# One-input Newton steps, first weights subtracted on VectorE, and a residual moved behind two projections, in a two-layer decoder trunk

## The chip, the cores and the metric

The kernel runs on one core of a Trainium2 chip. The metric is the device time of one execution in microseconds (us). The engines are TensorE (PE in the profile; its weight loads are PEld), VectorE (DVE), ScalarE (ACT), GpSimd (POOL) and SyncE (SP), which here only issues loads. Each engine works through its own queue in order; semaphores connect the queues.

## The reference

x is 512 tokens by 1024 features, mem is 256 fixed tokens by 1024, everything in float32. After an input norm, two layers follow, each with three sub-layers in the form x <- LayerNorm(alpha * x + f(x)):

```python
def reference(x, mem, ln0_g, ln0_b, ...):
    h = layer_norm(x, ln0_g, ln0_b)
    for l in range(DEPTH):
        mix = hybrid_mixer(h, w_in[l], w_a2[l], b_a[l], conv_w[l], ..., w_mix_out[l])
        h = layer_norm(DEEPNORM_ALPHA * h + mix, ln1_g[l], ln1_b[l])
        xa = memory_cross_attention(h, mem, w_xq[l], w_xkv[l], w_xo[l])
        h = layer_norm(DEEPNORM_ALPHA * h + xa, ln2_g[l], ln2_b[l])
        ff = swiglu(h, w_ffn_in[l], w_ffn_out[l])
        h = layer_norm(DEEPNORM_ALPHA * h + ff, ln3_g[l], ln3_b[l])
    return h

def hybrid_mixer(h, ...):
    c_a, c_g, q, k, v, r, a_low = jnp.split(h @ w_in, cuts, axis=-1)
    u = causal_depthwise_conv(c_a * jax.nn.sigmoid(c_g), conv_w, conv_b)   # 31 taps, 512 channels
    u = jax.nn.silu(layer_norm(u, conv_ln_g, conv_ln_b))
    log_a = jax.nn.log_sigmoid(a_low @ w_a2 + b_a) / GATE_TAU
    o = gla_chunked(q, k, v, log_a)                                        # 4 heads, chunks of 64
    o = rms_norm(o, gla_norm_g) * jax.nn.silu(r)
    return jnp.concatenate([u, o], axis=-1) @ w_out
```

## The kernel before

Every matmul operand is split into a high part, rounded by ScalarE, and a low part, the difference: `split` (lines 100 to 102) is one ScalarE copy and one subtraction on the engine it is given. A product is three matmuls, `mm3` (lines 137 to 139): high by high, high by low, low by high.

Weights come in chunks of 128 x 1024 (512 KB). `wchunk` loads a chunk by SP's queue into one of four `raw` buffers, and splits it into one of four ring buffers (or a resident one). Which engine does the subtraction is a setting, `wlo_engines(...)`: the engines named there take the chunks in turn. It is set to `(POOL, DVE)` for the memory keys `mem_K` of layer 0, to `(POOL)` at the start of each layer's mixer (line 557), to `(POOL, DVE)` after the r projection, and to `(DVE)` for the cross-attention.

Tokens lie in four tiles h[0..3] of 128 x 1024. Large blocks (hT, qk, v, KT, gamma and beta rows `gb`, and so on) come from one pool of 15 equal buffers, `blk`. The instructions are ordered by a planner (the tile framework's scheduler, which plays a model of the engines and takes instructions by the order in which they were written, apart from sections of high or low priority). So the order on a queue can change wherever a change makes something ready earlier or later in that model.

The pieces that the change touches, in the order of the run:

- *Start.* The memory is transposed (mT), `mem_K` makes the keys in four pairs of chunks (w_xk), while the input norm runs at high priority (lines 509 to 528): statistics, `rstd_of`, normalization on ScalarE without gamma and beta, transposes, and per-feature gamma and beta on the transposed side, which gives hT (high and low).
- *The Newton steps.* `rstd_of(v, n, name)` makes 1/sqrt of n columns per token row on VectorE: an integer start (line 147), t = y*v*y (lines 151 to 154), and products of the form (x + c) * z (lines 157, 159, 160). n is 1 for the LayerNorms over tokens, 2 for the convolution's norm, 8 for the RMS norm of the attention.
- *The mixer.* `conv_in(0)` (weights w_c, four chunks: g, then a), `conv_taps(0)` (62 multiply-adds on VectorE at low priority, line 590), `gates()`, `conv_in(1)`, `conv_taps(1)`, the k and q projections (w_qk, four chunks), transposes of kd, the v projection (w_v, four chunks), states S, `gla_pair(0)` with the first half of the r projection (w_r, four chunks), the rest of r, memory values (w_xv, eight chunks), then `conv_norm()` and `gla_pair(1)` at high priority, and the output projection (w_mo), whose results are added to h at line 273.
- *The residual.* The first sub-layer of layer 0 needs the input norm's output with gamma and beta, token-wise. `residual0()` (lines 530 to 534) loads gamma and beta, broadcast to 128 rows, with two loads on SP's queue into one of the 15 buffers, then does four multiplications and four additions of 128 x 1024 on GpSimd. It is called behind the transposes of kd, ahead of the v projection.
- *Between the layers.* The last norm of layer 0 (`layer_norm`, lines 174 to 202, names `y_ln`, `t_ln`, `s_ln`) produces the hT of layer 1, for which `conv_in(0)` of layer 1 waits. That `conv_in` works in two halves of tokens, so its first half needs only the first two token tiles.

Of the kernel before, what the change touches and what calls it, by code (L numbers as in the profile page):

```python
# [17 lines left out]
ALU = mybir.AluOpType  # L18
# [33 lines left out]
def trunk(ctx: ExitStack, tc, a, out):  # L52
    nc = tc.nc
    PE, ACT, DVE, POOL = nc.tensor, nc.scalar, nc.vector, nc.gpsimd
# [18 lines left out]
    def block(shape, dt, name):  # L73
        return blk.tile(shape, dt, tag="b", name=name)
# [25 lines left out]
    def split(hi, lo, src, eng=DVE):  # L100
        ACT.activation(hi, src, AF.Copy)  # L101
        eng.tensor_sub(lo, src, f(hi))  # L102
# [3 lines left out]
    def wlo_engines(*engs):  # L106
        wlo[0], wlo[1] = engs, 0
# [6 lines left out]
    def new_hT(name):  # L114

        return [[block([P, 4, T], F32R, f"hT{j}{i}_{name}") for i in range(2)] for j in range(2)]

    def mov_hT(hT):
        return lambda kt: (hT[0][kt // 4][:, kt % 4, :], hT[1][kt // 4][:, kt % 4, :])
# [21 lines left out]
    def rstd_of(v, n, name):  # L141


        y = small.tile([P, n], F32, tag=f"ny{n}", name=f"y_{name}")
        t = small.tile([P, n], F32, tag=f"nt{n}", name=f"t_{name}")
        s = small.tile([P, n], F32, tag=f"ns{n}", name=f"s_{name}")
        DVE.tensor_scalar(y.bitcast(I32), v.bitcast(I32), -0.5, 1597463007.0 - 2.0 ** 31, ALU.mult, ALU.add)

        def vyy():
            if n > 1:  # L150
                DVE.tensor_mul(t, y, v)
                DVE.tensor_mul(t, t, y)
            else:
                DVE.scalar_tensor_tensor(t, y, v, y, ALU.mult, ALU.mult)

        vyy()
        DVE.scalar_tensor_tensor(y, t, -3.0, y, ALU.add, ALU.mult)
        vyy()
        DVE.scalar_tensor_tensor(s, t, -40.0 / 3.0, t, ALU.add, ALU.mult)
        DVE.scalar_tensor_tensor(y, s, 80.0, y, ALU.add, ALU.mult)  # L160
        return y

    def bcast_row(dst, src_row, n, q):
# [2 lines left out]
    def load_gb(g, b, name, q=nc.sync):  # L166
        gb = block([P, 2, D], F32, f"gb_{name}")
        bcast_row(gb[:, 0, :], g, D, q)
        bcast_row(gb[:, 1, :], b, D, q)
        return gb  # L170
# [4 lines left out]
    def layer_norm(tt, st, gb, name, hT=None, store=None):  # L175
        ht = h[tt]
        mv = small.tile([P, 2], F32, tag="mv", name=f"mv_{name}{tt}")
        DVE.bn_aggr(mv, st)
        v = small.tile([P, 1], F32, tag="v", name=f"v_{name}{tt}")
        DVE.tensor_scalar(v, mv[:, 1:2], EPS, VS, ALU.add, ALU.mult)  # L180
        tail = store is not None and tt == NT - 1
        for i in range(2):
            s = slice(i * 512, (i + 1) * 512)
            DVE.scalar_tensor_tensor(
                ht[:, s], ht[:, s], mv[:, 0:1], gb[:, 0, s], ALU.subtract, ALU.mult)
        y = rstd_of(v, 1, f"{name}{tt}")
        for i in range(2):
            for c0 in range(i * 512, (i + 1) * 512, 256 if tail else 512):
                s = slice(c0, c0 + (256 if tail else 512))
                DVE.scalar_tensor_tensor(ht[:, s], ht[:, s], y, gb[:, 1, s], ALU.mult, ALU.add)  # L190
                if store is not None:
                    (nc.scalar if c0 % 512 else nc.sync).dma_start(store[:, s], ht[:, s])
            if hT is None:
                continue
            pt = bank(f"lt_{name}{tt}_{i}", tag="tr")
            for k in range(4):
                c = (i * 4 + k) * P
                PE.transpose(pt[:, k * P:(k + 1) * P], ht[:, c:c + P], ident)
            pv = pt.rearrange("p (k t) -> p k t", k=4)
            if callable(hT):  # L200
                hT(i, tt, pv)
                continue
            ts_ = slice(tt * P, (tt + 1) * P)
            split(hT[0][i][:, :, ts_], hT[1][i][:, :, ts_], pv)

    def proj_feat(w, mov, specs, name, n=T, halves=False):

        work = []
        for si, (c0, ncol, evac) in enumerate(specs):
            kk = 1024 // ncol  # L210
            wcs = [wchunk(w[ci * kk * P:(ci + 1) * kk * P, c0:c0 + ncol], kk, ncol, f"{name}{si}{ci}")
                   for ci in range(NK // kk)]
            banks = [bank(f"pp_{name}{si}{m}") for m in range(ncol // P)]
            work.append((kk, wcs, banks, evac))
        parts = [(0, n // 2), (n // 2, n)] if halves else [(0, n)]
        for t0, t1 in parts:
            for kk, wcs, banks, evac in work:
                for ci, (wh, wl) in enumerate(wcs):
                    for m, bk in enumerate(banks):
                        ms = slice(m * P, (m + 1) * P)  # L220
                        for k in range(kk):
                            kt = ci * kk + k
                            mh, ml = mov(kt)
                            mm3(bk[:, t0:t1], wh[:, k, ms], wl[:, k, ms], mh[:, t0:t1],
                                ml[:, t0:t1], kt == 0, kt == NK - 1)
                if t1 == n:
                    with tc.high_priority(offset=HP):
                        for m, bk in enumerate(banks):
                            evac(m, bk[:, :n])
# [20 lines left out]
    def run(gen):  # L250
        for _ in gen:
            pass
# [204 lines left out]
    def mem_T(name):  # L457
        mT = [block([P, NK, MEM], F32R, f"mT{j}_{name}") for j in range(2)]
        mraws = block([P, 2, D], F32, f"mem_{name}")
        for mt in range(2):  # L460
            nc.sync.dma_start(mraws[:, mt, :], a["mem"][0, mt * P:(mt + 1) * P, :])
        for mt in range(2):
            mraw = mraws[:, mt, :]
            for i in range(2):
                pt = bank(f"mt{mt}{i}_{name}", tag="tr")
                for k in range(4):
                    PE.transpose(pt[:, k * P:(k + 1) * P], mraw[:, (i * 4 + k) * P:(i * 4 + k + 1) * P], ident)
                ks, ms_ = slice(i * 4, i * 4 + 4), slice(mt * P, (mt + 1) * P)
                split(mT[0][:, ks, ms_], mT[1][:, ks, ms_], pt.rearrange("p (k t) -> p k t", k=4))
        return lambda kt: (mT[0][:, kt, :], mT[1][:, kt, :])  # L470

    def new_K(l):
        return [block([P, NK, MEM], F32R, f"KT{j}_{l}") for j in range(2)]

    def mem_K(l, mT, KT, pr):
        proj_feat(a["w_xkv"][l], mT,
                  [(pr * 256, 256, lambda m, ps: split(KT[0][:, pr * 2 + m, :], KT[1][:, pr * 2 + m, :], ps))],
                  f"xk{pr}_{l}", n=MEM)
# [10 lines left out]
    def load_x(*tts):  # L489
        for tt in tts:  # L490
            nc.sync.dma_start(h[tt], a["x"][0, tt * P:(tt + 1) * P, :])
# [7 lines left out]
    lncol = const.tile([P, 2 * NK], F32, name="lncol")  # L499
    DVE.tensor_copy(lncol, pl[:, :2 * NK])  # L500
    KT = new_K(0)
    mem_K(0, mT, KT, 0)
    load_x(0, 1)
    mem_K(0, mT, KT, 1)
    load_x(2, 3)
    for pr in range(2, 4):
        mem_K(0, mT, KT, pr)
    hT = new_hT("ln0")
# [21 lines left out]
    def residual0():  # L530
        gb = load_gb(a["ln0_g"], a["ln0_b"], "ln0")
        for tt in range(NT):
            POOL.tensor_mul(h[tt], h[tt], gb[:, 0, :])
            POOL.tensor_add(h[tt], h[tt], gb[:, 1, :])
# [4 lines left out]
    for l in range(L):  # L539
# [14 lines left out]
        DVE.tensor_scalar(nba, chan[:, 0:2, CW + 3], -1.0, None, ALU.mult)  # L554
        gnorm = chan[:, 0, CW + 4:CW + 5]
        mov = mov_hT(hT)
        wlo_engines(POOL)


        u = block([P, 4, T], F32, n_("u"))  # L560
# [9 lines left out]
        def conv_in(half):  # L570
            def ev_g(m, ps):
                ACT.activation(u[:, half * 2 + m, :], ps, AF.Sigmoid)

            def ev_a(m, ps):
                DVE.tensor_mul(u[:, half * 2 + m, :], u[:, half * 2 + m, :], ps)

            proj_feat(w_in, mov, [(CD + half * 256, 256, ev_g), (half * 256, 256, ev_a)], n_(f"c{half}"),
                      halves=half == 0 and l > 0)
# [55 lines left out]
            DVE.tensor_copy(dec, qe[:, :, CH - 1::CH])  # L634

        conv_in(0)
        if l > 0:
            mT = mem_T(f"{l}")
            KT = new_K(l)
# [13 lines left out]
        for hp in range(2):  # L653
# [1 line left out]
            for tt in range(NT):  # L655
                PE.transpose(pt[:, tt * P:(tt + 1) * P], kd[:, hp, tt * P:(tt + 1) * P], ident)
            ACT.activation(kdT[:, hp].rearrange("p a b -> p (a b)"), pt, AF.Copy)
        if l == 0:
            residual0()
        v = block([P, NT, 512], F32, n_("v"))  # L660
        run(proj_tok(w_in, mov, 1536, lambda tt, ps: ACT.activation(v[:, tt, :], ps, AF.Copy), n_("v")))

# [3 lines left out]
        for g in range(2):  # L666
# [12 lines left out]
            for cc in range(4):  # L679
                c, pu = g * 4 + cc, pus[cc % 2][:, cc // 2]  # L680
# [116 lines left out]
            mem_K(l, mT, KT, 0)  # L797
        gla_pair(0)
        run(proj_r)
        wlo_engines(POOL, DVE)  # L800
        for pr in range(1, 4) if l > 0 else ():
            mem_K(l, mT, KT, pr)
# [126 lines left out]
```

## Time and profile before

| | before |
|---|---|
| median of 3 runs | 1446.42 us (1444.23 to 1446.85) |
| profiled execution | 1448.14 us, span 1446.4 us |
| TensorE busy | 1405.3 us (97%) |
| VectorE busy | 1015.9 us (70%) |
| ScalarE busy | 608.8 us (42%) |
| GpSimd busy | 218.8 us (15%) |
| granted TensorE clock, mean | 0.992 |

A row of the order of time gives start, duration (both us; for several instructions in a row, from the first's start to the last's end), engine, line, operation, output<-inputs, shapes and count, and in brackets the idle time before it with what ended it. A row of waits gives who waited for what: total us, times, longest. A row of a stretch gives the busy time of PE, PEld, DVE, ACT and POOL, each with a count, the granted TensorE clock, the DMA engines' busy share and GB/s. Line numbers are those of the kernel before; a helper's line, such as 102, stands for all who call it, so the tile's name tells them apart.

### The profile page before, as it was taken

What the parts mean: (1) busy time and instruction counts of PE and PEld (TensorE: products, weight loads), DVE (VectorE), ACT (ScalarE), POOL (GpSimd) and SP (SyncE); (2) the same over time, 40 slices, a digit from 0 to 9 for tenths busy, and PEclk for the clock granted to TensorE, in tenths of its full rate; (3) what the DMA queues carried; (4) which work ended last, traced back from release to release, by engine and by line L of the source; (5) the groups of instructions that cost most, each with busy time, mean ns of one, the idle gap of its engine ahead of it and who ended that gap; (6) DMA issues with size and microseconds to landing.
All of it is one profiled execution on the core that took longest, in us unless ns stands there. A gap on an engine that the chain in (4) does not pass through costs nothing.

```text
span 1446.4 us, 22112 instructions
## 1 busy us (share of the span) xinstructions
PE 1405.3 (97%) x8943; PEld 1257.2 (87%) x8943; DVE 1015.9 (70%) x1674; ACT 608.8 (42%) x976; POOL 218.8 (15%) x124
## 2 busy tenths in 40 slices
PE   8999999999999999999979999999999999999997
PEld 7787878988999899899877888889889998998996
DVE  6699977557877367466859997685578664763767
ACT  5553362442555155245225335424424542561550
POOL 3467230000000000000133423300000000000000
PEclk9999999999999999999989999999999999999999
DMA  7423250221365265545242323612214662643641
GB/s 248 131 79 117 88 190 25 95 86 58 97 161 170 76 168 131 147 113 128 84 126 84 93 85 115 217 59 88 76 51 119 164 190 59 161 135 114 146 132 58
DMA packets 108730, 168.62 MB, mean 117 GB/s; under 512 B 7485, under 2 KB 81937, under 8 KB 108629
## 3 DMA queue, kind: packets, MB, share of 16 engines
q1 hardware_dynamic: 102548, 145.98, 32.1%
q0 software_dynamic: 5760, 20.97, 7.8%
q8 instruction: 70, 1.15, 0.3%
q14 instruction: 32, 0.25, 0.1%
q10 hardware_dynamic: 320, 0.27, 0.1%
HBM read 144.13 MB, written 2.10 MB: 101 GB/s over the span
## 4 chain that ended last, share of the span: by engine, by line
PE 76%; DVE 14%; DMA 5%; ACT 3%; issue 2%; POOL 0%; SPq 0%; DVEq 0%; POOLq 0%; ACTq 0%
DVE cv L590 6%; PE po_fo L137 5%; PE po_fo L138 5%; PE po_fo L139 5%; PE fx L402 5%; PE fx L404 5%; PE fx L403 5%; DMA s<-raw_a 3%; PE fw L404 2%; PE fw L403 2%; PE fw L402 2%; PE pp_xq L137 2%; PE pp_xq L138 2%; PE pp_xq L139 2%; PE po_mo L139 2%
## 5 line engine op out<-in xcount | busy, mean ns | idle before, releaser
L284 POOL DMA_DIRECT2D s<-raw_a x40 | 34.9, 885 | 873.4 <-DVE w_s L102 256.1
L590 DVE SCALAR_TENSOR_TENSOR cv<-u,chan,cv 128x511 f32<-128x511 f32 (+28 forms) x240 | 158.6, 728 | 0.3
L138 PE MATMUL po_fo<-w_fo,ph 128*128 128x512 f32 (+1 forms) x358 | 138.1, 386 | 0.0
L139 PE MATMUL po_fo<-w_fo,pl 128*128 128x512 f32 (+1 forms) x358 | 137.0, 386 | 0.0
L137 PE MATMUL po_fo<-w_fo,ph 128*128 128x512 f32 (+1 forms) x358 | 131.7, 386 | 0.0
L101 ACT ACTIVATE w_a<-raw_a 128x1024 fp32r<-128x1024 f32 x60 | 63.2, 1054 | 150.6 <-PE po_fo L139 124.6
L102 DVE TENSOR_TENSOR w_s<-s,w_s 128x1024 fp32r<-128x1024 f32 x80 | 97.3, 1220 | 33.3 <-ACT w_s L101 33.0
L101 ACT ACTIVATE w_s<-s 128x1024 fp32r<-128x1024 f32 x80 | 83.8, 1052 | 48.0 <-DMA s<-raw_a 27.6
L402 PE MATMUL fx<-T_ln,w_s 128*128 128x256 f32 x320 | 91.6, 287 | 3.5 <-ACT u L415 3.3
L403 PE MATMUL fx<-T_ln,w_s 128*128 128x256 f32 x320 | 91.2, 285 | 0.0
L404 PE MATMUL fx<-T_ln,w_s 128*128 128x256 f32 x320 | 90.6, 285 | 0.0
L273 DVE SCALAR_TENSOR_TENSOR h<-h,po_fo 128x512 f32<-128x512 f32 (+1 forms) x49 | 32.3, 671 | 71.2 <-PE po_fo L139 71.1
L102 DVE TENSOR_TENSOR w_a<-raw_a,w_a 128x1024 fp32r<-128x1024 f32 x60 | 73.0, 1220 | 9.1 <-ACT w_a L101 8.1
L139 PEld LDWEIGHTS po_fo<-w_fo,pl 128*128 128x128 f32 x358 | 67.3, 188 | 13.3
L138 PEld LDWEIGHTS po_fo<-w_fo,ph 128*128 128x128 f32 x358 | 67.3, 188 | 13.0
L137 PEld LDWEIGHTS po_fo<-w_fo,ph 128*128 128x128 f32 x358 | 66.9, 188 | 12.9
L402 PEld LDWEIGHTS fx<-T_ln,w_s 128*128 128x128 f32 x320 | 62.2, 194 | 4.2 <-ACT u L415 3.7
L102 DVE TENSOR_TENSOR w_fo<-raw_fo,w_fo 128x1024 fp32r<-128x1024 f32 x44 | 52.8, 1219 | 13.6 <-ACT w_fo L101 13.6
L403 PEld LDWEIGHTS fx<-T_ln,w_s 128*128 128x128 f32 x320 | 62.2, 194 | 0.0
L404 PEld LDWEIGHTS fx<-T_ln,w_s 128*128 128x128 f32 x320 | 61.8, 194 | 0.0
L138 PE MATMUL pp_xq<-hT_ln,w_xq 128*128 128x256 f32 (+1 forms) x192 | 61.3, 322 | 0.0
L139 PE MATMUL pp_xq<-hT_ln,w_xq 128*128 128x256 f32 (+1 forms) x192 | 60.3, 319 | 0.0
(315 smaller groups left out, 4478.3 us busy)
## 6 DMA issues: line engine op xcount, KB each, us to landing
raw_a<-w_ffn_in SPq DMA_DIRECT2D x60, 512.0 KB
raw_fo<-w_ffn_out SPq DMA_DIRECT2D x44, 512.0 KB
s<-raw_a POOLq DMA_DIRECT2D x40, 512.0 KB, 4.9
s<-w_ffn_in SPq DMA_DIRECT2D x20, 512.0 KB
raw_xk<-w_xkv SPq DMA_DIRECT2D x16, 512.0 KB
raw_c<-w_in SPq DMA_DIRECT2D x16, 512.0 KB
raw_xv<-w_xkv SPq DMA_DIRECT2D x16, 512.0 KB
raw_mo<-w_mix_out SPq DMA_DIRECT2D x16, 512.0 KB
```

What stands on the lines that cost most here:

```text
L101: ACT.activation(hi, src, AF.Copy)
L102: eng.tensor_sub(lo, src, f(hi))
L137: PE.matmul(o, lh, rh, start=start, stop=False)
L138: PE.matmul(o, lh, rl, start=False, stop=False)
L139: PE.matmul(o, ll, rh, start=False, stop=stop)
L273: DVE.scalar_tensor_tensor(h[tt][:, c0:c1], h[tt][:, c0:c1], scale, bks[c][:, :c1 - c0], ALU.mult, ALU.add)
L284: POOL.dma_start(dst, src, accum_op=ALU.add)
L402: PE.matmul(o, wh, bh, start=start and k == 0, stop=False, skip_group_check=True)
L403: PE.matmul(o, wh, bl, start=False, stop=False, skip_group_check=True)
L404: PE.matmul(o, wl, bh, start=False, stop=stop and k == 3, skip_group_check=True)
L590: DVE.scalar_tensor_tensor(cv[ct][:, s:], u[:, ct, :T - s], wj, cv[ct][:, s:], ALU.mult, ALU.add)
```

## The change

There are three edits. In `rstd_of`, for one column (n == 1), each Newton step is a `tensor_scalar` with one tensor input and the other factor as a per-row pointer operand, instead of a `scalar_tensor_tensor` with two tensor inputs; for 2 and 8 columns nothing changes. The low parts of the first memory-key chunks (two, of which GpSimd did the first) and of the four w_c chunks of `conv_in(0)` in each layer are subtracted on VectorE; from `conv_in(1)` on GpSimd has them as before. And `residual0()` is called behind the r projection instead of ahead of the v projection.

```diff
@@ rstd_of
-                DVE.scalar_tensor_tensor(t, y, v, y, ALU.mult, ALU.mult)
+                DVE.tensor_scalar(t, y, v, y, ALU.mult, ALU.mult)
+
+        def step(o, x, c, z):
+            if n > 1:
+                DVE.scalar_tensor_tensor(o, x, c, z, ALU.add, ALU.mult)
+            else:
+                DVE.tensor_scalar(o, x, c, z, ALU.add, ALU.mult)
 
         vyy()
-        DVE.scalar_tensor_tensor(y, t, -3.0, y, ALU.add, ALU.mult)
+        step(y, t, -3.0, y)
         vyy()
-        DVE.scalar_tensor_tensor(s, t, -40.0 / 3.0, t, ALU.add, ALU.mult)
-        DVE.scalar_tensor_tensor(y, s, 80.0, y, ALU.add, ALU.mult)
+        step(s, t, -40.0 / 3.0, t)
+        step(y, s, 80.0, y)
@@ start
     KT = new_K(0)
+    wlo_engines(DVE)
     mem_K(0, mT, KT, 0)
+    wlo_engines(POOL, DVE)
     load_x(0, 1)
@@ each layer
         mov = mov_hT(hT)
-        wlo_engines(POOL)
+        wlo_engines(DVE)
...
         conv_in(0)
+        wlo_engines(POOL)
         if l > 0:
...
-        if l == 0:
-            residual0()
         v = block([P, NT, 512], F32, n_("v"))
...
         gla_pair(0)
         run(proj_r)
+        if l == 0:
+            residual0()
         wlo_engines(POOL, DVE)
```

## The prediction

> **What bounds the kernel now.** I read the page first (spans, then the chain that ended last), then TensorE's waits stretch by stretch, then the order of time of single engines around each wait.
>
> ```profile
> span 1446.4 us, 22112 instructions
> PE 1405.3 (97%) x8943; PEld 1257.2 (87%) x8943; DVE 1015.9 (70%) x1674; ACT 608.8 (42%) x976; POOL 218.8 (15%) x124
> PE 76%; DVE 14%; DMA 5%; ACT 3%; issue 2%; POOL 0%; SPq 0%; DVEq 0%; POOLq 0%; ACTq 0%
> ```
>
> TensorE is busy 97% of the span, so a change outside it pays only where TensorE stands still or runs slowly. The view of waits, one stretch after another, says where that is near the edited lines:
>
> ```profile
> PE lt_ln L198 <- DVE hT_ln L102: 4.0, 1, 4.0
> PE pp_c L137 <- DVE h L273: 3.8, 1, 3.8
> ...
> PE pp_c L138 <- DVE hT_ln L102: 2.9, 2, 1.7
> ...
> PE pt_v L137 <- DVE qk L646: 1.9, 1, 1.9
> PE pp_qk L139 <- POOL w_qk L102: 0.8, 2, 0.6
> ```
>
> (Columns: total us, times, longest.) The first two lie between the layers (700 to 760 us), the third in layer 0's first projection (0 to 60), the last two in its q/k and v projections (100 to 150). Together 13.4 us: the order of what can be won.
>
> **Part 1: between the layers.** The order of time of VectorE, GpSimd, ScalarE and TensorE there, with the clock by stretch:
>
> ```profile
> 719.86 1.86 DVE L157 SCALAR_TENSOR_TENSOR y_ln<-t_ln,y_ln 128x1 f32<-128x1 f32 x1
> 721.76 2.28 DVE L154 SCALAR_TENSOR_TENSOR t_ln<-y_ln,v_ln 128x1 f32<-128x1 f32 x1
> 724.07 2.27 DVE L159 SCALAR_TENSOR_TENSOR s_ln<-t_ln 128x1 f32<-128x1 f32 x1
> ...
> 726.86 2.15 DVE L160 SCALAR_TENSOR_TENSOR y_ln<-s_ln,y_ln 128x1 f32<-128x1 f32 x1
> ...
> 730.85 0.68 DVE L102 TENSOR_TENSOR hT_ln<-lt_ln,hT_ln 128x512 fp32r<-128x512 f32 x1
> ...
> 735.05 0.16 DVE L159 SCALAR_TENSOR_TENSOR s_ln<-t_ln 128x1 f32<-128x1 f32 x1
> ```
>
> ```profile
> 719.31 7.01 POOL L102 TENSOR_TENSOR w_c<-raw_c,w_c 128x1024 fp32r<-128x1024 f32 x3 [49.04 <-DVE hT_ln L102]
> ```
>
> ```profile
> 725.51 1.06 ACT L101 ACTIVATE w_c<-raw_c 128x1024 fp32r<-128x1024 f32 x1 [2.48 <-DMA raw_c<-w_in]
> ```
>
> ```profile
> 732.35 0.56 PE L138 MATMUL pp_c<-hT_ln,w_c 128*128 128x256 f32 x1
> ```
>
> ```profile
> 727.00:731.50 4.50, 0.57 (x1) 0.28 (x1) 4.50 (x6) 0.00 (x0) 1.99 (x1) 0.50 0.60 154
> 731.50:736.50 5.00, 4.92 (x23) 4.92 (x24) 4.18 (x15) 1.10 (x3) 0.00 (x0) 0.50 0.23 81
> ```
>
> ```profile
> L102 DVE TENSOR_TENSOR w_a<-raw_a,w_a 128x1024 fp32r<-128x1024 f32 x60 | 73.0, 1220 | 9.1 <-ACT w_a L101 8.1
> ```
>
> Four one-element Newton steps take 1.86 + 2.28 + 2.27 + 2.15 = 8.56 us while GpSimd subtracts the first weights w_c; the same step takes 0.16 when GpSimd is idle. Behind them on VectorE's queue stands the low half of the second token tile's hT (730.85), for which TensorE waits. With the four w_c subtractions gone from GpSimd the steps cost about 0.7, so 7.9 us of stall go (the narrower operands alone would do the same). In exchange VectorE takes four subtractions at 1.22: 4.9 us. If none stands ahead of that hT, TensorE restarts 7.9 us earlier; if all four do, 3.0 earlier. The fourth can't be early: its weights are rounded at 725.51 + 1.06 = 726.57, so a queue that holds hT behind it gives 726.57 + 1.22 + 2 x 0.68 = 729.2 against a restart at 732.35, 3.2 us. I expect the later-traced w_c subtractions to fill gaps in the norm's chain, about three ahead of the restart: 7.9 - 3.7 = 4.2, taken as **-4.5** (ends -3.0 and -7.9).
>
> The granted clock is 0.50 from 727 to 736.5, so some 4.9 us of matmuls ran at half speed: up to 2.4 us more if the pause becomes short. What pause costs the clock, this trace only brackets: two pauses of about 4 us did, while one of 1.7 (layer 0) left it at 1.00:
>
> ```profile
> 40.00:45.00 5.00, 3.21 (x13) 2.28 (x14) 5.00 (x5) 3.45 (x6) 5.00 (x3) 1.00 0.32 38
> ```
>
> I credit nothing, since 8 us of broken work shrink to about 4. The Trainium skill (TensorE: Matmul & The Clock Gate, Part 1) says that an idle window of about 3.4 us halves the clock and a busy one restores it; the rows fit, and by it a pause under that length would bring the 2.4 us too.
>
> **Part 2: start of layer 0.** The order of time of VectorE and GpSimd:
>
> ```profile
> 38.16 5.24 DVE L102 TENSOR_TENSOR hT_ln<-xf,hT_ln 128x512 fp32r<-128x512 f32 x2 [4.57 <-ACT hT_ln L101]
> ...
> 43.99 2.82 DVE L102 TENSOR_TENSOR hT_ln<-xf,hT_ln 128x512 fp32r<-128x512 f32 x2
> ...
> 47.28 0.69 DVE L102 TENSOR_TENSOR hT_ln<-xf,hT_ln 128x512 fp32r<-128x512 f32 x1
> ```
>
> ```profile
> 9.18 2.36 POOL L102 TENSOR_TENSOR w_xk<-raw_xk,w_xk 128x1024 fp32r<-128x1024 f32 x1 [6.38 <-ACT w_xk L101]
> 14.71 2.39 POOL L102 TENSOR_TENSOR w_xk<-raw_xk,w_xk 128x1024 fp32r<-128x1024 f32 x1 [3.17 <-ACT w_xk L101]
> ...
> 37.68 7.97 POOL L102 TENSOR_TENSOR w_c<-raw_c,w_c 128x1024 fp32r<-128x1024 f32 x3 [2.68 <-PE lt_ln L525]
> ```
>
> Four hT subtractions take 8.06 us beside GpSimd's w_c where 4 x 0.69 = 2.8 would do. That frees 5.3 us of VectorE and puts back 4 x 1.22 = 4.9, but VectorE idled 4.57 before them, so the first w_c fit ahead. Of TensorE's 2.9 us here I take **-2.0** (ends 0 and -2.9). The first w_xk chunk, 2.36 on GpSimd, is 1.22 on VectorE: 1.1 at best; as VectorE has two other subtractions there, **-0.5** (ends +0.3 and -1.1).
>
> ```profile
> 16.03 0.27 DVE L147 TENSOR_SCALAR y_ln<-v_ln 128x1 int32<-128x1 int32 x2
> 16.22 1.02 DVE L154 SCALAR_TENSOR_TENSOR t_ln<-y_ln,v_ln 128x1 f32<-128x1 f32 x2
> ```
>
> These two stand beside the 14.71 row of GpSimd: the one-input tensor_scalar ran at 0.135 each, the two-input form waited. So the Newton edit does what it says for one column. I cost it at nothing here: TensorE multiplies the memory keys without a wait while the input norm runs. If that cover is gone, it is worth the excess of this row, 0.7 us, and as much as one GpSimd subtraction, 2.4, for each further hit.
>
> Where GpSimd is idle, the edit gives three more steps of each chain a pointer operand:
>
> ```profile
> 1440.98 0.22 DVE L154 SCALAR_TENSOR_TENSOR t_ln<-y_ln,v_ln 128x1 f32<-128x1 f32 x1
> 1441.24 0.16 DVE L157 SCALAR_TENSOR_TENSOR y_ln<-t_ln,y_ln 128x1 f32<-128x1 f32 x1
> ```
>
> The step that has one takes 0.22, the other 0.16: 3 x 0.06 = **+0.2** on the last row of the output norm, where nothing hides it (ends 0 and +0.5, if two pointers cost twice).
>
> **Part 3: the residual.** It leaves this place, here with VectorE's scan in layer 0 and in layer 1, which has no residual:
>
> ```profile
> 90.71 11.40 POOL L533 TENSOR_TENSOR h<-h,gb_ln 128x1024 f32<-128x1024 f32 x4
> ```
>
> ```profile
> 87.34 4.49 DVE L627 TENSOR_TENSOR_SCAN dk<-reset,qk 128x512 f32<-128x512 f32 x2
> ...
> 785.22 3.25 DVE L627 TENSOR_TENSOR_SCAN dk<-reset,qk 128x512 f32<-128x512 f32 x2
> ```
>
> GpSimd's third w_qk no longer queues behind four multiplications: TensorE's 0.8 us on w_qk go. The scan may lose 1.2 us, though w_qk subtractions move up into its place; the 1.9 us on L646 stand behind VectorE's convolution taps, which start earlier with part 2. I take **-1.8** (ends 0 and -2.8, all of both waits). Also moved are its two broadcast loads of 512 KB on SP's queue, past the loads of w_v and w_r: those issue that much sooner, and hide under their buffers' waits as now.
>
> In its new place, after r and ahead of V's weights on GpSimd:
>
> ```profile
> 157.86 2.38 POOL L102 TENSOR_TENSOR w_xv<-raw_xv,w_xv 128x1024 fp32r<-128x1024 f32 x1 [13.35 <-ACT w_xv L101]
> ```
>
> ```profile
> 220.34 1.37 DVE L273 SCALAR_TENSOR_TENSOR h<-h,po_mo 128x512 f32<-128x512 f32 x2 [3.83 <-PE po_mo L139]
> ```
>
> ```profile
> 867.10 2.34 DVE L151 TENSOR_TENSOR t_rms<-y_rms,ms 128x8 f32<-128x8 f32 x1
> ```
>
> GpSimd has 13.35 us free before the first w_xv, and gaps between the later ones; h is first read at 220.34. The work is 11.40 for the multiplications and, at about 2.4 each like w_xv, 9.6 for the additions: 21 us, of which some 8 spill past 157.86. Then a w_xv can wait up to 2.9 for its turn, and the Newton steps of the RMS and convolution norms, which keep two inputs (8 and 2 columns), can each lose 2.34 - 0.17 = 2.2, as in layer 1 at 867. I charge **+1.5**, two thirds of one such hit (ends 0 and +17, all eight operations hitting one).
>
> **Sum.** -4.5 - 2.0 - 0.5 + 0.2 - 1.8 + 1.5 = -7.1 us. The profiled execution took 1448.14 us, 1.7 above its span and 1.7 above the median 1446.42 of three runs; on it the sum gives 1441.0, and on the median **1439.3**.
>
> **The rivals.** *VectorE's queue waits for weights.* The order puts a w_c subtraction ahead of the norm while its weights are still on the way (ScalarE idled 2.48 for the DMA at 725.51). Then part 1 brings 3.0 and part 2 perhaps 0.5: with the rest -4.1, so about 1442.3. For it: the queue is in order and GpSimd no longer takes that wait; against: only the fourth chunk is late.
>
> *The residual lands on the norms, slower than before.* The gains and rents leave -8.6 without the new place's charge. The residual's gamma and beta take one of 15 large buffers; while r runs, mT, KT, hT, u, qk, dk, v, S and gr hold 14. If cOh gets the last, the loads wait until r ends and hT is free, and the eight operations run over the Newton steps of both norms, whose results (og, csl) TensorE waits for in order. Each hit costs 2.2: the change turns slower from the fourth on (8.8 against 8.6), and eight make 17.4 - 8.6 = +8.8, so 1455.2. Against it: dk falls free before r ends. The Trainium skill (SBUF — State Buffer, SBUF: two separate sides) calls the port that VectorE and GpSimd share an exclusive lock held for the whole instruction; 2.34 for 0.17 of work agrees, and by it no hit is cheaper than what is left of the GpSimd operation.
>
> *It breaks even.* Four hits: -8.6 + 8.8 = +0.2, 1446.6.
>
> **How the numbers follow.** Forecast 0.62, waiting queue 0.12, break-even 0.12, residual on the norms 0.14. Within 0.2% (2.9 us, about what a measurement can tell) is the third case alone: faster 0.74, same 0.12, slower 0.14. All good ends at once give 7.9 + 2.4 + 2.9 + 1.1 + 2.8 = -17.1 (1429.3), unlikely together, so the low end is 1432; the high end, 1448, takes in break-even. The likeliest case alone: 1432 to 1443.5.
>
> **What would show it.** Right: no Newton step of one column over 0.3 us anywhere; TensorE back on pp_c of layer 1 by the equivalent of 728, its waits there under 5 us; hT of layer 0 at 0.7 each; no wait on w_qk; the residual done before V's last w_xv. Wrong: VectorE idle on ScalarE's w_c between the layers; steps of 8 or 2 columns at 2 us in layer 0 beside GpSimd's h; TensorE waiting for og, csl or a late h at po_mo.

## The result, and the profile after

The changed kernel took 1455.9 us (median of 4 runs, 1453.16 to 1458.71); the kernel before took 1445.5 beside it. The ratio is 1.0072 [1.0047, 1.0097]: slower by 0.7%, where 1439.3 was forecast. Its profiled execution took 1454.29 us, at a mean granted clock of 0.989. (Line numbers up to 154 are as before, later ones lie up to 8 higher: the one-column norm steps are now lines 154 and 160, the two- and eight-column ones 151, 152 and 158, the residual 541 and 542. In the experiments they differ by a few lines again, so go by the tiles' names.)

The page's span and chain:

```profile
span 1452.6 us, 22117 instructions
PE 70%; DVE 17%; DMA 6%; ACT 3%; issue 3%; POOL 0%; SPq 0%; DVEq 0%; POOLq 0%; ACTq 0%
```

VectorE's share of the chain rose from 14 to 17%. GpSimd has none, although it is what VectorE waits for: a held instruction is recorded as a long one, not as a wait.

TensorE's waits, in this order between the layers (700 to 780 us), at the start (0 to 60) and around the norms of layer 0 (150 to 235):

```profile
PE pp_c L137 <- DVE h L279: 1.5, 1, 1.5
...
PE lt_ln L533 <- ACT xf L535: 2.3, 1, 2.3
...
PE po L767 <- DVE attT L757: 10.5, 1, 10.5
PE cvb L728 <- ACT acc L722: 5.2, 1, 5.2
PE ogt L797 <- DVE og L793: 2.0, 2, 1.7
```

The two waits of 7.8 us between the layers became one of 1.5, as meant. At the start one wait (2.9) gave way to another (`lt_ln`, 2.3). The loss is the third group, which before held no wait over 1.1. The order of time there, SP's queue, then GpSimd, then VectorE:

```profile
128.57 40.73 SPq L125 DMA_DIRECT2D raw_xv<-w_xkv  x8
172.55 8.04 SPq L125 DMA_DIRECT2D raw_mo<-w_mix_out  x3
180.64 0.42 SPq L170 DMA_DIRECT2D gb_ln<-ln_g  x1
181.11 0.42 SPq L170 DMA_DIRECT2D gb_ln<-ln_b  x1
```

```profile
151.12 2.39 POOL L102 TENSOR_TENSOR w_xv<-raw_xv,w_xv 128x1024 fp32r<-128x1024 f32 x1 [13.99 <-ACT w_xv L101]
...
188.25 9.30 POOL L541 TENSOR_TENSOR h<-h,gb_ln 128x1024 f32<-128x1024 f32 x4
197.52 3.31 POOL L542 TENSOR_TENSOR h<-h,gb_ln 128x1024 f32<-128x1024 f32 x1
200.79 2.35 POOL L102 TENSOR_TENSOR w_mo<-raw_mo,w_mo 128x1024 fp32r<-128x1024 f32 x1
203.10 6.95 POOL L542 TENSOR_TENSOR h<-h,gb_ln 128x1024 f32<-128x1024 f32 x3
```

```profile
188.35 2.32 DVE L147 TENSOR_SCALAR y_cln<-v 128x2 int32<-128x2 int32 x1
190.70 2.27 DVE L151 TENSOR_TENSOR t_cln<-y_cln,v 128x2 f32<-128x2 f32 x1
193.01 2.26 DVE L152 TENSOR_TENSOR t_cln<-t_cln,y_cln 128x2 f32<-128x2 f32 x1
195.19 3.44 DVE L102 TENSOR_TENSOR w_mo<-raw_mo,w_mo 128x1024 fp32r<-128x1024 f32 x1
198.56 2.29 DVE L158 SCALAR_TENSOR_TENSOR y_cln<-t_cln,y_cln 128x2 f32<-128x2 f32 x1
...
203.19 2.27 DVE L152 TENSOR_TENSOR t_cln<-t_cln,y_cln 128x2 f32<-128x2 f32 x1
205.50 2.26 DVE L158 SCALAR_TENSOR_TENSOR s_cln<-t_cln 128x2 f32<-128x2 f32 x1
207.80 2.26 DVE L158 SCALAR_TENSOR_TENSOR y_cln<-s_cln,y_cln 128x2 f32<-128x2 f32 x1
```

The gamma and beta loads stand behind all eight w_xv and three w_mo loads on SP's queue. So GpSimd lets its 13.99 us gap pass and does the residual from 188 to 210. There the convolution norm's second half runs on VectorE, and its steps take 2.26 to 2.32 us each. GpSimd's operations follow each other without a pause, and each held step ends about as one of them does: seven steps are held for 2.1 us each, a w_mo subtraction for another 2.2. ScalarE's normalizing passes (`acc`, one row for each half, first before, then after) show what that makes:

```profile
183.03 1.93 ACT L715 ACTIVATE acc<-cvt,b,y_cln 128x256 f32<-128x256 f32 x4 [3.67 <-DVE b L711]
197.35 1.93 ACT L715 ACTIVATE acc<-cvt,b,y_cln 128x256 f32<-128x256 f32 x4 [4.41 <-DVE b L711]
...
179.84 1.93 ACT L722 ACTIVATE acc<-cvt,b,y_cln 128x256 f32<-128x256 f32 x4 [5.28 <-DVE b L718]
210.29 1.93 ACT L722 ACTIVATE acc<-cvt,b,y_cln 128x256 f32<-128x256 f32 x4 [20.56 <-DVE b L718]
```

The second half follows the first by 14.3 us before and 30.5 after: 16.1 more. Behind the pauses the clock falls too:

```profile
195.00:200.00 5.00, 0.00 (x0) 0.00 (x0) 5.00 (x3) 0.00 (x0) 5.00 (x3) 0.63 0.14 13
200.00:205.00 5.00, 3.20 (x15) 3.23 (x16) 4.88 (x7) 0.00 (x0) 5.00 (x3) 0.50 0.24 92
```

### The profile page after: what moved, and what is told of

It is laid out like the page before. It is cut to its first block, busy times and chain, and to the rows that moved or that the text cites. A ratio compares the mean times of both kernels' runs of the same rounds, so it can differ in the third digit from the quotient of the medians.

```text
span 1452.6 us, 22117 instructions
## 1 busy us (share of the span) xinstructions
PE 1404.8 (97%) x8943; PEld 1256.0 (86%) x8943; DVE 1033.5 (71%) x1683; ACT 608.7 (42%) x976; POOL 195.1 (13%) x115
## 4 chain that ended last, share of the span: by engine, by line
PE 70%; DVE 17%; DMA 6%; ACT 3%; issue 3%; POOL 0%; SPq 0%; DVEq 0%; POOLq 0%; ACTq 0%
DVE cv L598 8%; PE po_fo L137 5%; PE po_fo L138 5%; PE po_fo L139 5%; PE fx L408 5%; PE fx L409 4%; PE fx L410 4%; DMA s<-raw_a 3%; PE fw L409 2%; PE fw L410 2%; PE fw L408 2%; PE pp_xq L138 2%; PE pp_xq L137 2%; PE pp_xq L139 2%; PE po_xo L139 2%
## 5 line engine op out<-in xcount | busy, mean ns | idle before, releaser
L598 DVE SCALAR_TENSOR_TENSOR cv<-u,chan,cv 128x511 f32<-128x511 f32 (+29 forms) x240 | 158.8, 735 | 0.2
```

Of the source, the lines that this page charges most:

```text
L598: DVE.scalar_tensor_tensor(cv[ct][:, s:], u[:, ct, :T - s], wj, cv[ct][:, s:], ALU.mult, ALU.add)
```

## The experiments

Three sets ran, each set on one chip with the kernel before beside it (medians of before 1445.24, 1444.67 and 1444.75); every ratio is against that. The times are medians of 4 to 12 runs, and a ratio's interval of 0.15% is about 2 us. The theory: GpSimd's eight residual operations, in the place that they got, hold VectorE one for one (A). The rivals: what the change does to VectorE's queue (B), the loads and their block, or the place of the call.

**1. Which part costs.** The changed kernel with `residual0()` back in its old place, everything else kept; and the kernel before with only the residual moved.

```diff
 e1_residual_back (from after)      e2_residual_only (from before)
+        if l == 0:                -        if l == 0:
+            residual0()           -            residual0()
         v = block(...)                     v = block(...)
...
         run(proj_r)                        run(proj_r)
-        if l == 0:                +        if l == 0:
-            residual0()           +            residual0()
```

> The changed kernel with residual0() called at its old place, ahead of the v projection; the other two edits stay. Theory A (the changed kernel loses its time only because GpSimd's eight residual operations, from 188 to 210 us, hold up the two-column Newton steps of the convolution norm): the steps run at 0.2 us again, TensorE's waits of 10.5 and 5.2 us there go, and the gains at the start and between the layers stay: about 1436, 9 under the kernel before. Rival B (the first weights on VectorE cost the time, by VectorE's load): at or above 1446.

> The kernel before with residual0() moved behind the r projection, nothing else. Theory A: the residual again runs over the convolution norm's second half, 8 hits of about 2.2 us: some 15 to 18 us slower than before, about 1461. Rival B: within 3 us of before, 1443 to 1448.

Residual back: 1438.83, ratio 0.9953 [0.9938, 0.9969]. Only the residual moved: 1461.77, ratio 1.0114 [1.0100, 1.0128], with TensorE's 10.5 and 5.2 us waits again. The move costs 17.1 with the other two parts (1455.9 - 1438.8) and 16.5 without (1461.8 - 1445.2); the other two bring 6.4. B is out.

What leaving the old place is worth is read from the residual moved alone. TensorE's waits on w_qk and on qk (0.8 and 1.9 us) are gone, and its first w_r subtraction came 4.4 us earlier than before, but the norm's first pass came at the same time (before: 183.03):

```profile
183.01 1.93 ACT L713 ACTIVATE acc<-cvt,b,y_cln 128x256 f32<-128x256 f32 x4 [3.66 <-DVE b L709]
213.44 1.93 ACT L713 ACTIVATE acc<-cvt,b,y_cln 128x256 f32<-128x256 f32 x4 [20.52 <-DVE b L709]
```

VectorE's convolution taps end at 168.6 before and at 167.8 here, and the norm waits for them (TensorE's first transposes for the norm now wait 1.8 us for `acc`, which the taps fill): the time won ahead of them is used up there.

**2. Arithmetic or loads.** The changed kernel with the eight operations cut to one column, then to half their width; loads and calls stay. (The operations are 1024 wide in each row; where the texts say 512 and 256 columns, 1024 and 512 are meant. Each of the two loads is 512 KB, not 1 MB.)

```diff
-            POOL.tensor_mul(h[tt], h[tt], gb[:, 0, :])
+            POOL.tensor_mul(h[tt][:, :1], h[tt][:, :1], gb[:, 0, :1])          # e14; e15: [:, :D // 2]
...
```

> The changed kernel with its two 1 MB of gamma and beta loads and every call where they were, but GpSimd's eight residual operations cut from 512 columns to one (the rest of the residual is left out). Theory A, the eight operations alone cost the time, each holding one of VectorE's norm operations: they become too short to hold anything, the second half of the convolution norm takes the 14.3 us that it takes before (first ACT pass of one half to the next) and not 30.5, and the time falls to that of the kernel with the residual back in its old place, 1438.8 (1437 to 1442). Theory B, the loads cost it, by the block they hold and by their place on SP's queue: they stand as before, so 1450 or more.

> The changed kernel with loads and calls in their place and each of the eight residual operations on 256 of the 512 columns of a row tile pair, half of their elements (the other half of the residual is left out). Theory A, one held VectorE operation for each GpSimd operation, for as long as that runs: the operations take 1.2 us and not 2.3, the second half of the convolution norm starts its ACT pass some 22 us after the first (14 at one column, 30.5 at full width), and the time is midway between 1439.3 and 1455.9: 1445 to 1450. Rival G, the cost is of the switch between the engines or of the clock's fall, not of the length: 1453 to 1456.

One column: 1439.34, ratio 0.9959 [0.9943, 0.9974]. Half width: 1446.21, ratio 1.0007 [0.9997, 1.0017]. In the half-width kernel, GpSimd, VectorE and ScalarE:

```profile
193.31 5.00 POOL L541 TENSOR_TENSOR h<-h,gb_ln 128x512 f32<-128x512 f32 x4
...
193.42 1.22 DVE L147 TENSOR_SCALAR y_cln<-v 128x2 int32<-128x2 int32 x1
194.67 1.21 DVE L151 TENSOR_TENSOR t_cln<-y_cln,v 128x2 f32<-128x2 f32 x1
195.91 1.19 DVE L152 TENSOR_TENSOR t_cln<-t_cln,y_cln 128x2 f32<-128x2 f32 x1
...
184.92 1.94 ACT L722 ACTIVATE acc<-cvt,b,y_cln 128x256 f32<-128x256 f32 x4 [3.66 <-DVE b L718]
206.94 1.93 ACT L722 ACTIVATE acc<-cvt,b,y_cln 128x256 f32<-128x256 f32 x4 [12.11 <-DVE b L718]
```

The passes lie 13.8 us apart at one column (182.25 and 196.09), 22.0 at half and 30.5 at full width: 8.2 and 8.4 for each half, 16.6 in all or 2.1 per full operation. A held step lasts as long as the GpSimd operation beside it (1.2 for 5.00 / 4, 2.3 for 9.30 / 4). Rival G, a cost that doesn't go by the length, is out. The loads, which stand in their late place in both, cost nothing that shows.

**3. What sets the place.** Call after r as in the change, but gamma and beta in other buffers: one small-weight and one raw buffer, then two raw staging buffers. And the large block kept, with the call moved ahead of the second gate pair, behind the states S.

```diff
-        gb = load_gb(a["ln0_g"], a["ln0_b"], "ln0")
+        gam = quarter([P, D], "gam_ln0")           # e13; e16: a second "raw" tile
+        bet = stage.tile([P, D], F32, tag="raw", name="bet_ln0")
...
# e9_after_S, with gb as in the change:
+        if l == 0:
+            residual0()
         cUh = block([P, 4, T], F32R, n_("cUh"))
```

> The changed kernel, with the called place of the residual as it is (after r), but gamma and beta loaded into a buffer of the small weights' kind and one raw staging buffer, not one of the 15 large blocks. Theory A, the late place came from the wait for a block: the loads then go out among the w_xv weights and the eight operations stand between those subtractions, well before the second half of the convolution norm, as in the kernel called after S (1442.0): 1438 to 1444. Rival C, the place of the call itself sets the late start: the residual still stands at about 188 us, 1453 to 1458. Rival D, a raw buffer held by beta delays the w_xv weights behind it: each w_xv multiplication waits up to two loads, 1446 to 1452.

> The changed kernel with the residual called after r as it is, and gamma and beta loaded into two of the raw staging buffers that every weight passes through, not into one of the 15 large blocks. Theory A, what GpSimd's late start waits for is the block: the loads then follow raw_r on SP's queue at about 133 us, the eight operations stand among the w_r and w_xv subtractions at about 130 to 160 us, beside convolution taps, and no small norm operation is held: 1437 to 1443. Rival C, the place of the call sets it: the operations stand at 172 us or later and the time is 1453 to 1458.

> The changed kernel with residual0() called behind the states S, ahead of r. There its load is placed after three of the w_xv loads, and the residual stands on GpSimd between the last w_r and the first w_xv, the idle stretch that the prediction counted on. Theory A: no two-column step is hit, both other gains stay, and the start keeps w_qk free of the residual: 1431 to 1437. Rival C: like the changed kernel if the late load is what costs, 1450 or more.

One small and one raw buffer: 1455.6, ratio 1.0069 [1.0054, 1.0084]. Neither A's place nor C's, and above D's range: beta was loaded at 133.56, but gamma only at 166.53 behind five w_xv loads, so the residual stood at 172, where the RMS norm's eight-column steps took the hits, and TensorE waited 17.1 us for og:

```profile
172.26 10.43 POOL L544 TENSOR_TENSOR h<-h,gam_ln 128x1024 f32<-128x1024 f32 x4 [7.25 <-DMA gam_ln<-ln_g]
...
185.04 2.27 DVE L158 SCALAR_TENSOR_TENSOR y_rms<-t_rms,y_rms 128x8 f32<-128x8 f32 x1
...
187.34 2.27 DVE L151 TENSOR_TENSOR t_rms<-y_rms,ms 128x8 f32<-128x8 f32 x1
...
PE ogt L800 <- DVE og L796: 17.1, 1, 17.1
```

Another victim and the same bill. Two raw buffers: 1438.78, ratio 0.9958 [0.9944, 0.9972]. The call stands where the change has it, and the operations 55 us earlier:

```profile
129.64 0.35 SPq L170 DMA_DIRECT2D gam_ln<-ln_g  x1
132.36 0.35 SPq L170 DMA_DIRECT2D bet_ln<-ln_b  x1
...
133.07 9.46 POOL L544 TENSOR_TENSOR h<-h,gam_ln 128x1024 f32<-128x1024 f32 x4 [0.74 <-DMA gam_ln<-ln_g]
```

So with the call where it is, the large block is what makes the late place. Called behind S: 1442.04, ratio 0.998 [0.997, 0.9991], five above what A gave and far below the changed kernel. The residual ran from 145.28, beside convolution taps and without a held norm step; the norm's passes lie 15.2 us apart against 14.3 before, and the layer boundary gained as in the others. So the block alone doesn't make the place late either: it takes the block and a call behind r. That the wait for a free block does it is inferred from these swaps and not seen, because the changed kernel's SP queue does not stop at the gamma load (it follows the load ahead of it by 0.05 us); the planner had put it there. Why this run stayed 3 us above the residual back in its old place is open: its profile does not show it (its span, 1440.2, is 0.9 shorter than that one's, which is the slowest of its five runs).

**4. Take the victim away.** The convolution norm's two-column chain cut into one-column chains with one tensor input, in the changed kernel, and in the one with the residual back.

```diff
-                DVE.tensor_scalar(v2, mv2[:, :, 1], EPS, VS, ALU.add, ALU.mult)
-                y2 = rstd_of(v2, 2, n_(f"cln{g}"))
...
+                for i in range(2):
+                    DVE.tensor_scalar(v2[:, i:i + 1], mv2[:, i, 1:2], EPS, VS, ALU.add, ALU.mult)
+                    y2.append(rstd_of(v2[:, i:i + 1], 1, n_(f"cln{g}{i}")))
+                    DVE.tensor_scalar(b2[:, i:i + 1], mv2[:, i, 0:1], y2[i], -1.0, ALU.mult, ALU.mult)
```

> The changed kernel, residual in its new place, with the convolution norm's Newton steps done one column at a time with one tensor input each (twelve steps per pair of token tiles instead of eight). Theory A (steps with two inputs, or with two columns, wait for GpSimd's operation; one-input one-column steps don't): the steps run at about 0.2 us under the same GpSimd work, so 12 to 17 us come back: 1439 to 1444. Rival C (the late load of gamma and beta delays the output projection's weights, not the port): no better than the changed kernel, 1453 to 1458.

> The changed kernel with the residual in its old place (1438.8 in an earlier run) and the convolution norms' two-column chains cut into one-column chains with one tensor input. Theory A, in this kernel nothing holds the two-column chains for long, so there is nothing left to gain there, and eight more small operations for each norm half lie on the path: 1438 to 1442. Rival H, the w_xv subtractions of GpSimd still hold some of them: 1434 to 1437.

In the changed kernel: 1446.91, ratio 1.0012 [1.0002, 1.0022], between the two expectations. The norm's last steps run beside the residual unheld (0.33 for two); the earlier ones now come before it starts at 191.46, so part of the gain is the planner's new order. The passes are 11.1 us apart. But the residual then meets the subtractions of cUl and the RMS norm's steps, and TensorE waits there:

```profile
191.46 11.45 POOL L541 TENSOR_TENSOR h<-h,gb_ln 128x1024 f32<-128x1024 f32 x4 [2.95 <-DMA gb_ln<-ln_g]
...
192.50 0.33 DVE L160 TENSOR_SCALAR s_cln<-t_cln 128x1 f32<-128x1 f32 x2
...
206.72 5.69 DVE L102 TENSOR_TENSOR cUl<-csl,cUh 128x512 fp32r<-128x512 f32 x2
...
218.00 2.27 DVE L147 TENSOR_SCALAR y_rms<-ms 128x8 int32<-128x8 int32 x1
...
PE ogt L799 <- DVE og L795: 11.3, 1, 11.3
```

A was half right: it left out the other two-input operations behind the chain, which are victims as well. With the residual back: 1433.51, ratio 0.9921 [0.9906, 0.9935], the fastest of all. My expectation said nothing was left to gain; the rival's number (1434 to 1437) was nearer. Its two passes, and TensorE's clock and work in that stretch (before: 18.47 of 20 us):

```profile
181.33 1.94 ACT L726 ACTIVATE acc<-cvt,b,y_cln 128x256 f32<-128x256 f32 x4 [2.96 <-DVE b L722]
192.48 1.93 ACT L726 ACTIVATE acc<-cvt,b,y_cln 128x256 f32<-128x256 f32 x4 [0.62 <-DVE b L722]
...
180.00:200.00 20.00, 19.87 (x158) 15.83 (x157) 17.30 (x46) 15.73 (x25) 6.34 (x4) 1.00 0.60 182
```

11.2 us apart and not 14.3. GpSimd had held one of the two-column steps here before, too (the step of line 157 took 1.47), but beside a w_mo subtraction and not a w_xv one, and that is 1.3 of the 3.2 us. The rest came with a new order on VectorE's queue: the second half's statistics follow the first pass after 4.1 us, not 5.4. How much of the gain is the form of the steps and how much the order was not separated.

**5. The layer boundary.** The kernel before with the Newton edit alone, and with the weights alone.

```diff
 e5_newton_only: rstd_of as in the change; wlo_engines and residual0() as before
 e6_weights_only: wlo_engines as in the change; rstd_of and residual0() as before
```

> The kernel before with only the Newton steps of one-column norms given one tensor input; the first weights and the residual stay on GpSimd where they were. Theory E, the boundary's loss was VectorE's Newton steps held by GpSimd's w_c subtractions (five of 1.86 to 2.28 us where 0.16 to 0.22 is their time alone): with one tensor input they are not held, the waits of 4.0 and 3.8 us at the layer boundary go, 1438 to 1441. Rival F, the steps with a pointer operand are held as the ones with two tensor inputs were (the two-column TENSOR_SCALAR with one tensor input took 2.32 us beside GpSimd): the waits stay and the time is 1444 to 1447.

> The kernel before with only w_c and the first w_xk subtracted on VectorE; Newton steps and residual as they were. Theory E: with GpSimd idle at the layer boundary nothing holds the two-input Newton steps, VectorE pays 3 x 1.2 us for the w_c subtractions that it takes over ahead of the norm, and the gain is the same as with both parts but for that: 1438 to 1442. Rival F, both parts are needed: w_c on VectorE stands ahead of the Newton steps and the norm waits as long as before: 1444 to 1448.

Newton alone: 1440.04, ratio 0.9965 [0.9953, 0.9976], as E said (four steps were held in the kernel before, not five). Weights alone: 1442.24, ratio 0.9976 [0.9963, 0.9989], 0.2 above E's range. F is out in the first; in the second the time alone leaves it possible, but the waits of 4.0 and 3.8 are gone (0.9 is left). From GpSimd's clearing of layer 1's attT (657.5 in before) to layer 1's first w_qk (771.0) the profiles gain 8.1 and 6.4 us, against 6.1 in the changed kernel and 7.0 with the residual back: each part takes nearly all of the boundary alone, and they don't add. (With the residual alone moved, the same stretch gains 0.1.) The times of the two show less, 4.6 and 2.4 us; where the rest went is open, as single profiles differ by some us in layer 0 as well. With the Newton edit alone the next victim shows:

```profile
726.84 5.30 DVE L190 SCALAR_TENSOR_TENSOR h<-h,mv_ln,gb_ln 128x512 f32<-128x512 f32 x2
```

Two operations of 0.7 on h take 5.30 beside w_c, but TensorE waits only 1.3 for them.

## Why the prediction was wrong, step by step

*The residual's new place (+1.5) is the step that failed.* It put the work where it is called, "after r and ahead of V's weights on GpSimd", and charged two thirds of one hit. Measured: 16.1 us between the norm's halves, 17.1 in the time, the end of the charged range (+17, all eight operations hitting one). The price of a hit was right (2.2 charged, 2.1 found). The condition stood in the rival "the residual lands on the norms", loads waiting for a block till r ends, and was right in part: r's last matmul ended at 164.6, and the loads came 16 us later still, behind weights. That rival gave 1455.2; 1455.9 was measured, in part by luck: it stood for 8.8 us of loss, where 10.4 were measured against a kernel before that ran 0.9 faster beside it, and it had the steps of both norms held, where only the convolution norm's second half was. I gave it 0.14 because dk falls free before r ends. That a block falls free does not decide which tile gets it. The loads in two raw buffers show that the block mattered, but which tile took the last block on the way was not tried. The range's high end, 1448, left that case out.

*The residual's old place (-1.8): about 0.* The waits that were to go did go, and GpSimd's queue did run 4 us ahead, but the convolution taps on VectorE bound the stretch. The residual at one column, 1439.34, is no faster than the residual in its old place, 1438.83: in its old place it costs nothing that these times can tell (they can tell about 3 us), so no move of it could gain more than that.

*Between the layers (-4.5): -6 to -8.* The direction was right and the size too small. Three w_c subtractions stand ahead of the second tile's hT, as expected, but the planner now takes that hT ahead of the rest of the norm's chain, so the pause lost 6.3 us and not 4.2: it fell from 7.8 to 1.5. The clock that I did not credit came back in part: from 725 to 735, at the end of the boundary, before and with the residual back,

```profile
725.00:735.00 10.00, 4.00 (x17) 3.71 (x18) 9.93 (x18) 2.15 (x4) 3.67 (x2) 0.56 0.48 121
...
725.00:735.00 10.00, 8.55 (x57) 8.36 (x58) 9.51 (x24) 1.67 (x3) 0.00 (x0) 0.83 0.75 216
```

A longest wait of 1.5 us still left it at 0.50 for 3 us (739 to 742 in the changed kernel), so not all of the 2.4 us came that the prediction names for a short pause.

*Start of layer 0 (-2.0 and -0.5): about -0.5, not settled.* Over the ten profiles with that part, the first w_qk of layer 0 came between 3.5 us earlier and 1.6 later than before, 0.5 earlier on the mean; but the three profiles without it lie 3.4 us apart themselves. hT's subtractions fell to 0.69 as predicted (all but one), but TensorE met the wait on `xf` (2.3) a step ahead, so its waits from 0 to 60 fell only from 8.9 to 8.3 us: what was late next was not asked. With the boundary's larger gain this may cancel: without the residual's move the sum gave -6.8, and -6.4 was measured, so that this number fits is in part luck.

*Newton steps of one column (+0.2).* No one-column step in the new form is over 0.28 us anywhere in the changed kernel; where GpSimd is idle the rows show 0.20 to 0.28 for 0.16 to 0.22, as charged.

## What to carry to other kernels

Before moving work to an engine with idle time, ask what its input needs first (a buffer, a load, a queue place): that, and not the line of the call alone, sets when it runs, and the gap that was counted on may be past by then. GpSimd work of n operations beside a chain of short VectorE operations costs up to n times the GpSimd operation, whatever the VectorE work is worth alone; so keep it beside operations that it does not hold (here those with one input in PSUM, or of one column), or give the chain such a form. A part that can win only where nothing waits for it (here the residual's old place) is best bounded first, by its cost in a kernel that leaves it out.

## What the runs showed of the hardware

I had expected two-input operations alone to be held. The two-column step of line 147 has one tensor input and took 2.32 us beside the residual (1.22 beside the half-width one); with one column the same step ran at 0.15 beside a w_mo subtraction, in the changed kernel with the norm cut into columns:

```profile
185.99 2.51 POOL L102 TENSOR_TENSOR w_mo<-raw_mo,w_mo 128x1024 fp32r<-128x1024 f32 x1 [5.14 <-ACT w_mo L101]
...
187.75 0.15 DVE L147 TENSOR_SCALAR y_cln<-v 128x1 int32<-128x1 int32 x1
```

The Trainium skill (VectorE: DVE Perf Modes, Mode 2×_2P) says that a single-source operation in SBUF streams one half of its tensor through each of the two read ports when its outermost dimension longer than one is even (or odd and equal in source and destination). Two columns meet that and one column leaves nothing to halve, and both rows agree. The prediction read the one-input form as free; it is the column count as well.

Nor are all two-input operations held. With the residual called behind S, the convolution taps beside it keep their 0.65 us:

```profile
145.28 9.43 POOL L541 TENSOR_TENSOR h<-h,gb_ln 128x1024 f32<-128x1024 f32 x4 [3.57 <-DMA gb_ln<-ln_g]
...
147.71 4.55 DVE L598 SCALAR_TENSOR_TENSOR cv<-u,chan,cv 128x495 f32<-128x495 f32 x7
```

Their running sum cv lies in a PSUM bank (the pool that the kernel's matmuls write to), and of the two tensors only u lies in SBUF (where its other tiles lie). The Trainium skill (SBUF — State Buffer, Who interferes with whom) says that a VectorE instruction with at most one SBUF input, outside the two-port modes, does not contend with GpSimd; these rows agree. That fits a residual that is harmless among the taps and costs 17 us among the norms; a kernel with cv in SBUF was not tried.
